# Output projection: three token tiles first, router sums through the fourth's bank, affine vectors loaded together; last expert pair: factor products behind the statistics

## The chip, the core and the metric

The program runs on one core of a Trainium2 chip. Its time is the device time in microseconds (us), the lower the better; three runs give a median. A traced run records what each engine did: PE (TensorE) multiplies matrices, and PEld is its loading of weights; DVE (VectorE), ACT (ScalarE) and POOL (GpSimd) work elementwise; SP (SyncE) here only issues transfers, which run on 16 DMA engines. The granted clock is the share of TensorE's full clock that the chip let it have.

## What is computed

The trunk has two layers over 512 tokens of 1024 numbers, and both end in the same kind of expert block. The part that matters is the end of the second mixer, its router and the experts behind it:

```
mix = (h * gelu(gate_br)) @ w_out                     # [512, 1024] @ [1024, 1024]
x = layer_norm(ALPHA * x + mix, ln_mix_g[1], ln_mix_b[1])
aff = softmax(x @ w_router[1])                        # 16 experts
gates, idx = top_k(aff.T, 64)                         # each expert takes 64 tokens
out_e = (silu(g) * u) @ w_down[e] * gates[e]          # g, u = split(x[idx[e]] @ w_gate_up[e])
x = layer_norm(ALPHA * x + scatter_add(out_e), ln_ffn_g[1], ln_ffn_b[1])
```

The input of the second layer is itself a normalised sum; its factor `ln_ffn_g[0]` and shift `ln_ffn_b[0]` are multiplied and added late, in `affine`, before the residual is taken.

## The kernel before

**Order.** The code is a Python program that emits instructions. Where two of them are independent, a scheduler in the compiler sets their order on each engine from costs of its own; each engine then runs its own list strictly in order, and waits at the head of it for whatever the head needs. `after(i, j)` puts `i` behind `j` by hand. Inside the expert pairs (from the second on) PE's order is the code's.

**Tiles.** Tokens lie in four tiles of 128 (`x[t]`, in rows of the trace `z` in the second layer). The accumulators of PE come from `bank(tag)`: four banks `A`, two `B`, two `C`, used in rotation.

**Output projection** (in `rglru`). The eight 128-row slices of `w_out` (`kk` in `ks`) are each split into a high and a low part (`wh` by ACT, `wl` by DVE), and each of the eight accumulators `acc[t, hf]` (tile, half of the columns; `wops` in rows) takes three products per slice: 192 in all. Before the change all eight accumulators get their banks at once, the first four slices go over all tiles, and then tile after tile takes its last four slices. DVE meanwhile does `affine`: it multiplies the four tiles by one vector, and adds the other. Both vectors pass through one buffer, `ffnvec`, so the second load (`ln_ffn_b`) is issued when the four products are done.

**Router.** `Router.prepare` transposes the vectors of the mixer's norm (`mixT`), scales the router's weights by them, and lets PE sum the columns (`rsums`); it is put behind the last product of the first four slices, and takes two `C` banks. `Router.finish` follows for each tile: statistics on DVE (`ln_mv`), eight transposes on PE (`rtp`), copies, the eight products with the router's weights (`logits`, two rows of the trace for each), and on DVE and ACT the softmax (`lg`, then the exponential on ACT, then `aff`). When all four tiles have their `aff`, `Router.first` ranks the tokens of the first two experts: `affb` on PE, four counting passes `junk` on DVE, then the selection matrix `oh`. With it PE gathers tokens (`gather`) and starts the first gate and up products (`gu`).

**Experts** (`moe`). Eight pairs of experts. Each pair reads 24 MB of weights, all issued on SP's list in one order; a load waits until the buffer that it goes to was read by PE. Some buffers of the first pair are the former `hgh` tiles of the output projection (`wgu000`, `wgu001`, `wgu100`, `wgu101`).

**Last pair.** The outputs are added half by half, and the last half in two quarters: `down` (`yp`), `weigh` (`ysb`, its high part on ACT, its low part on DVE), `spread` (`comb`), and on DVE the sum (`acc`) and the statistics (`bn_stats`). `scale` multiplies parts of `acc` by the last norm's factor, which is loaded behind all weights (`grow`). The list `V` of the flow also splits the factor and shift rows (`gbg`) into a high part (`gbgh`, ACT) and a low part (`gbgl`, DVE).

Of the kernel before, what the change touches and what calls it, by code (L numbers as in the profile page):

```python
# [11 lines left out]
F32 = mybir.dt.float32  # L12
# [6 lines left out]
P = 128  # L19
S = 512  # L20
D = 1024
# [12 lines left out]
NEG = -1e30  # L34
W2 = (8, 3)
BACC = {"dynamic_dma_scratch_size": 256}
TAGS = ('AABA', 'BAAB')
LORDER = 'C0 C1 R0 C2 R1 G0 C3 R2 G1 R3 G2 G3'
CONVT = 'BABCBCBB'
CONVE = 'AAAAADDD'  # L40
# [66 lines left out]
def trunk(ctx: ExitStack, tc: tile.TileContext, a: dict, out: bass.AP):  # L107
# [80 lines left out]
    class Router:  # L188
# [4 lines left out]
                nc.sync.dma_start(scratch[8 * i:8 * i + 8, :P], a[f"ln_mix_{nm}"][layer].rearrange("(c p) -> c p", p=P))  # L193
            self.scratch, self.layer = scratch, layer

        def prepare(self, behind=None):
            rows, ones, wb = self.scratch[:16, :P], self.scratch[:, P:2 * P], self.scratch[:, 2 * P:3 * P]
            part = self.scratch[:, 3 * P:3 * P + 2 * NE]
            ps = bank("C", name="mixT")
            mm = nc.tensor.transpose(ps[:, :16], rows, ident[:16, :16])  # L200
            if behind:
                after(mm, behind)
            gb = self.gb = cpool.tile([P, 16], F32, tag="mixT", name="mixT", bufs=2)
            nc.vector.tensor_copy(gb, ps[:, :16])
            nc.gpsimd.memset(ones, 1.0)
            wb = wb.rearrange("p (k e) -> p k e", k=KD)
            for i, w in ((1, wb), (0, self.w)):
                (nc.gpsimd if MIXE[i] == "P" else nc.vector).tensor_tensor(w, self.w, gb[:, i * KD:(i + 1) * KD, None].to_broadcast([P, KD, NE]), op=ALU.mult)
                nc.vector.tensor_reduce(part[:, i * NE:(i + 1) * NE], w.rearrange("p k e -> p e k"), axis=AX.X, op=ALU.add)
            ps = bank("C", name="rsums")[:, :2 * NE]  # L210
            nc.tensor.matmul(ps, ones, part, start=True, stop=True)
            self.sums = cpool.tile([P, 2, NE], F32, tag="rsums", name="rsums", bufs=2)
            nc.vector.tensor_copy(self.sums, ps.rearrange("p (a e) -> p a e", a=2))
            self.aff = cpool.tile([P, NT, NE], F32, tag="aff", name="aff", bufs=2)
            self.rank = cpool.tile([P, NT, 2], F32, tag="rank", name="rank", bufs=2)
# [372 lines left out]
    def rglru(es2, x, normed, w_in, w_r, w_i, w_out, prep):  # L588
        with ExitStack() as es:
# [128 lines left out]
                    nc.vector.tensor_tensor(hl[:, f, :], gt, hh.bitcast(F32)[:, f, :], op=ALU.subtract)  # L718
                hgh[n], hgl[n] = hh, hl

            def affine(pool):
                for nm, op in (("g", ALU.mult), ("b", ALU.add)):
                    v, src = pool.tile([P, D], F32, tag="ffnvec", name="ffnvec", bufs=1), a[f"ln_ffn_{nm}"][0]
                    nc.sync.dma_start(v, bass.AP(tensor=src.tensor, offset=src.offset, ap=[[0, P], [1, D]]))
                    for t in range(NT):
                        nc.vector.tensor_tensor(x[t], x[t], v, op=op)

            for c in LORDER.split():
                {"C": conv_block, "R": lru_block, "G": gate_branch}[c[0]](int(c[1]))
# [8 lines left out]
            for i in hgh:  # L738
                wts[i] = wtile([2, D], f"wout{i}")
                nc.sync.dma_start(wts[i], w_out[256 * i:256 * (i + 1), :].rearrange("(a p) d -> p a d", p=P))  # L740
            router = Router(p1b, alloc(), 1)
            for j, i in enumerate(hgh):
                for h in range(2):
                    ks.append(2 * i + h)
                    wo[2 * i + h] = split(p2 if j < 2 else p1b, wts[i][:, h, :], "A", WOE[2 * j + h], WB if j < 2 else 8)
            acc = {}
            for t in range(NT):
                for hf in range(2):
                    acc[t, hf] = bank("A" if t < 2 else "BC"[t - 2], name="wops")

            def out_mm(t, hf, kk):
                hs, ts_ = slice(hf * 512, (hf + 1) * 512), slice(t * P, (t + 1) * P)
                return mm3(acc[t, hf], hgh[kk // 2][:, kk % 2, ts_], hgl[kk // 2][:, kk % 2, ts_],
                           wo[kk][0][:, hs], wo[kk][1][:, hs], kk == ks[0], kk == ks[-1])

            for kk in ks[:4]:
                for t in range(NT):
                    for hf in range(2):
                        mm = out_mm(t, hf, kk)
            affine(p1b)  # L760
            router.prepare(mm)
            for t in (int(c) for c in TORD):
                for hf in range(2):
                    for kk in ks[4:]:
                        out_mm(t, hf, kk)
                    hs = slice(hf * 512, (hf + 1) * 512)
                    nc.vector.scalar_tensor_tensor(x[t][:, hs], x[t][:, hs], ALPHA, acc[t, hf], op0=ALU.mult, op1=ALU.add)
                router.finish(x[t], t, alloc, TAGS[1][t])
# [3 lines left out]
    def moe(x, layer, w_gu, w_dn, routing, emit):  # L772
        aff = routing.aff
        with ExitStack() as es:
# [5 lines left out]
            for p in range(NPAIR):  # L780
# [108 lines left out]
                for op in flow:  # L889
                    ks, es = ([int(c) for c in w] for w in (op[1:] + ":01").split(":")[:2])  # L890
                    if op[0] == "G":
                        gather(ks, es)
                    elif op[0] == "U":
                        gate_up(ks, es)
                    elif op[0] == "X":
                        tail = ks
                    elif op[0] == "W":
                        combine_weights()
                    elif op[0] == "C":
                        combine(ks)  # L900
                    elif op[0] == "P":
                        routing.positions(sel[0])
                    elif op[0] == "V":
                        grow = xpool.tile([P, D], F32, tag="act", name="grow", bufs=NT)
                        rows = xpool.tile([P, D], F32, tag="act", name="gbg", bufs=NT)[:3]
                        gbg = [xpool.tile([P, D], F32R, tag="act", name="gbg" + s, bufs=NT)[:3] for s in "hl"]
                        gsrc, bsrc = (a[f"ln_ffn_{nm}"][1] for nm in "gb")
                        end = after(nc.sync.dma_start(grow, bass.AP(tensor=gsrc.tensor, offset=gsrc.offset, ap=[[0, P], [1, D]])), end)
                        for i, src in enumerate((gsrc, bsrc, gsrc)):
                            end = after(nc.sync.dma_start(rows[i:i + 1, :], src.rearrange("(o d) -> o d", o=1)), end)  # L910
                        nc.scalar.copy(gbg[0], rows)
                        nc.vector.tensor_tensor(gbg[1], rows, gbg[0].bitcast(F32), op=ALU.subtract)
                        mcol = cpool.tile([P, NT, 3], F32, tag="mixT", name="mcol", bufs=2)
                        nc.gpsimd.memset(mcol, 1.0)
                h = gpool.tile([P, FF], F32, tag="hy", name="h", bufs=2)
# [63 lines left out]
                if last:  # L979
# [9 lines left out]
                    for i, (n, cols) in enumerate(((0, slice(0, 512)), (1, halves[0]))):  # L989
# [4 lines left out]
                        for t in range(NT):  # L994
                            ps = bank("C", name="comb")[:, :cols.stop - cols.start]
                            spread(ps, t, n, cols)
                            nc.vector.tensor_tensor(acc[t][:, ns], acc[t][:, ns], ps, op=ALU.add)
                            nc.vector.bn_stats(sts[t][:, i, :], acc[t][:, ns])
                        for t, j in (((0, 0), (1, 0)), ((0, 1), (1, 1), (2, 1), (3, 1), (2, 0)))[i] if emit else ():
                            scale(t, (slice(0, 512), slice(512, 768))[j])  # L1000
                    down(1, range(KD), halves[1])
                    weigh(1, halves[1])
                    for t in range(NT):
# [93 lines left out]
```

## Time and profile before

| what | value |
|---|---|
| median of 3 runs | 1405.56 us (1404.56 to 1405.69) |
| the traced execution | 1406.57 us, of which 1404.8 us from the first to the last instruction |
| share of that span busy | PE 96%, DVE 41%, ACT 25%, POOL 5% |
| chain of work that ended last | PE 82%, DMA 10%, DVE 4%, ACT 3% |
| mean granted TensorE clock | 0.977 |

The chain is followed back from the last instruction: at each step it goes to whatever released it. A row of the timeline merges neighbours of one kind: start, length, engine, line, operation, output and input tiles, count, and in brackets the idle time ahead of it with its releaser.

### The profile page before, as it was taken

The numbers are of one execution on the slowest core, as the hardware profiler recorded it, in microseconds if no ns is written. First come the engines' busy times: TensorE is split into PE (matmuls) and PEld (weight loads), VectorE is DVE, ScalarE is ACT, GpSimd is POOL, SyncE is SP. The second block draws the span as 40 slices with busy tenths as digits, with TensorE's granted clock in tenths as the row PEclk, the third lists the DMA queues.
The fourth block names the chain that finished last, engine by engine and source line by source line (L and its number), as shares of the span: only waits on it lengthen the run. The fifth ranks groups of instructions, "written<-read, shape, count | busy, mean of one in ns | idle before, by whom it ended". The sixth has DMA issues, their size and how long they took to land.

```text
span 1404.8 us, 17589 instructions
## 1 busy us (share of the span) xinstructions
PE 1354.5 (96%) x7015; PEld 770.4 (55%) x7015; DVE 574.4 (41%) x1293; ACT 345.7 (25%) x671; POOL 66.6 (5%) x105
## 2 busy tenths in 40 slices
PE   7998998999999999999799999999999999999996
PEld 7986776453453553544466668854553543544533
DVE  4586868232220230211556887762240211212206
ACT  5455332111010010110336883211010110111110
POOL 3142320000000000000000000000000000000000
PEclk9999998999999999999899999889999999999997
DMA  5134357979999999999931327648999999999992
GB/s 189 64 82 129 142 225 285 367 323 421 420 419 421 421 420 421 420 421 409 376 105 60 119 91 270 275 171 346 377 420 420 420 420 420 419 420 420 420 388 96
DMA packets 93095, 437.31 MB, mean 311 GB/s; under 512 B 10315, under 2 KB 37203, under 8 KB 46422
## 3 DMA queue, kind: packets, MB, share of 16 engines
q1 hardware_dynamic: 93014, 436.20, 78.0%
q8 instruction: 55, 0.90, 0.3%
q14 instruction: 26, 0.21, 0.0%
HBM read 434.07 MB, written 2.10 MB: 310 GB/s over the span
## 4 chain that ended last, share of the span: by engine, by line
PE 82%; DMA 10%; DVE 4%; ACT 3%; issue 1%; SPq 0%; POOL 0%; ACTq 0%; DVEq 0%; POOLq 0%
PE gu L867 28%; PE yp L952 14%; PE gather L851 8%; DMA wgu<-in_moe_w_gate_up_dram 4%; DMA wdn<-in_moe_w_down_dram 4%; PE comb L964 4%; PE gps L660 3%; PE wops L183 2%; PE wops L185 2%; PE wops L184 2%; PE qkv L185 2%; PE qkv L183 2%; PE qkv L184 1%; PE logits L229 1%; PE po L483 1%; PE htp L928 1%
## 5 line engine op out<-in xcount | busy, mean ns | idle before, releaser
L867 PE MATMUL gu<-wgu,xs 128*64 128x512 f32 x2048 | 460.5, 595 | 1.2 <-ACT xs L857 1.2
L867 PEld LDWEIGHTS gu<-wgu,xs 128*64 128x64 f32 x2048 | 146.5, 137 | 284.1 <-issue 272.8
L952 PE MATMUL yp<-wdn,hT 128*64 128x512 f32 (+1 forms) x1088 | 232.1, 574 | 2.4 <-DMA wdn<-in_moe_w_down_dram 2.4
L921 DVE TENSOR_TENSOR h<-h,gu 128x512 f32<-128x512 f32 x32 | 22.0, 687 | 356.7 <-PE gu L867 305.2
L952 PEld LDWEIGHTS yp<-wdn,hT 128*64 128x64 f32 x1088 | 78.0, 139 | 139.0 <-issue 127.5
L960 DVE SCALAR_TENSOR_TENSOR ysb<-yp,gate,ysb 128x512 fp32r<-128x512 f32 (+1 forms) x34 | 24.4, 719 | 217.5 <-ACT ysb L959 217.5
L920 ACT ACTIVATE h<-gu 128x512 f32<-128x512 f32 x32 | 19.0, 597 | 300.2 <-PE gu L867 300.2
L857 ACT ACTIVATE xs<-gather,mixT 128x128 f32<-128x128 f32 (+1 forms) x74 | 33.5, 455 | 199.5 <-DVE xs L859 134.5
L964 PE MATMUL comb<-ysb,cs 128*128 128x512 f32 (+1 forms) x256 | 68.7, 406 | 7.8 <-DVE ysb L960 3.8
L972 DVE TENSOR_TENSOR acc<-acc,comb 128x512 f32<-128x512 f32 x112 | 71.6, 682 | 0.7
L851 PEld LDWEIGHTS gather<-oh,z 128*128 128x128 f32 x520 | 60.2, 192 | 13.0 <-issue 10.8
L851 PEld LDWEIGHTS gather<-oh,x 128*128 128x128 f32 x520 | 60.3, 192 | 11.7 <-issue 8.9
L959 ACT ACTIVATE ysb<-yp,gate 128x512 fp32r<-128x512 f32 (+1 forms) x34 | 22.5, 662 | 175.1 <-PE yp L952 175.1
L851 PE MATMUL gather<-oh,z 128*128 128x128 f32 (+1 forms) x520 | 62.8, 278 | 1.6 <-DVE oh L829 1.6
L851 PE MATMUL gather<-oh,x 128*128 128x128 f32 (+1 forms) x520 | 63.0, 278 | 0.3 <-DVE pos L326 0.3
L183 PE MATMUL qkv<-wh,xh 128*128 128x256 f32 x192 | 55.3, 289 | 3.6 <-ACT wh L175 3.6
L660 PE MATMUL gps<-xc,wg 128*128 128x512 f32 x128 | 56.5, 593 | 1.5 <-ACT xc L638 1.5
L964 PEld LDWEIGHTS comb<-ysb,cs 128*128 128x128 f32 x256 | 45.6, 192 | 20.8 <-ACT ysb L959 5.5
L185 PE MATMUL qkv<-wh,xl 128*128 128x256 f32 x192 | 56.2, 293 | 0.0
L184 PE MATMUL qkv<-wl,xh 128*128 128x256 f32 x192 | 55.5, 290 | 0.7 <-DVE wl L176 0.7
L859 DVE TENSOR_SCALAR xs<-gather,mixT 128x128 f32<-128x128 f32 x56 | 22.9, 408 | 60.3 <-PE gather L851 60.3
L929 ACT COPY hT<-htp 128x512 f32<-128x512 f32 x32 | 18.7, 585 | 106.1 <-PE htp L928 106.1
(262 smaller groups left out, 1776.1 us busy)
## 6 DMA issues: line engine op xcount, KB each, us to landing
wgu<-in_moe_w_gate_up_dram SPq DMA_DIRECT2D x252, 1024.0 KB, 19.8
wdn<-in_moe_w_down_dram SPq DMA_DIRECT2D x124, 1024.0 KB, 18.9
win<-in_lru_w_in_dram SPq DMA_DIRECT2D x8, 1024.0 KB, 5.5
wqkv<-in_attn_w_qkv_dram SPq DMA_DIRECT2D x12, 512.0 KB, 4.5
wo<-in_attn_w_o_dram SPq DMA_DIRECT2D x16, 256.0 KB, 5.0
wgu<-in_moe_w_gate_up_dram SPq DMA_DIRECT2D x8, 512.0 KB, 4.1
wdn<-in_moe_w_down_dram SPq DMA_DIRECT2D x8, 512.0 KB, 10.5
wout<-in_lru_w_out_dram SPq DMA_DIRECT2D x4, 1024.0 KB, 7.3
```

The costliest lines, as they stand in the source:

```text
L183: nc.tensor.matmul(ps, lh, rh, start=start, stop=False)
L184: nc.tensor.matmul(ps, lh, rl, start=False, stop=False)
L185: return nc.tensor.matmul(ps, ll, rh, start=False, stop=stop)
L660: nc.tensor.matmul(ps, wt[:, 2 * z + gi, kk, fs], xc[n][:, kk, :], start=(kk == 0), stop=(kk == 1))
L851: pe(nc.tensor.matmul(ps[:, i, cols], x[t][:, k * P:(k + 1) * P], oh[:, t, es[0]:es[-1] + 1, :].rearrange("p e s -> p (e s)"), start=(t == ...
L857: nc.scalar.activation(xs[:, k, cols], ps[:, i, cols], AF.Identity, bias=bc, scale=gc)
L859: nc.vector.tensor_scalar(xs[:, k, cols], ps[:, i, cols], gc, bc, op0=ALU.mult, op1=ALU.add)
L867: pe(nc.tensor.matmul(gu[n][e * 64:(e + 1) * 64, :], xs[:, k, e * 64:(e + 1) * 64], wgu[e][k][n // 2][:, n % 2 * 512:(n % 2 + 1) * 512], s ...
L952: pe(nc.tensor.matmul(yp[n][e * 64:(e + 1) * 64, cols], hT[:, k, e * 64:(e + 1) * 64], w, start=(k == 0), stop=(k == KD - 1)))
L960: nc.vector.scalar_tensor_tensor(lo, yp[n][:, cols], gate, hi.bitcast(F32), op0=ALU.mult, op1=ALU.subtract)
L964: pe(nc.tensor.matmul(ps, cs[:, t, :], y[n][:, j, cols], start=start and not j, stop=bool(j)))
L972: nc.vector.tensor_tensor(acc[t][:, ns], acc[t][:, ns], ps, op=ALU.add)
```

## The change

In the output projection a tile's two accumulators get their banks when its first product is emitted, and the first three slices go over tiles 0 to 2 only. Then come `router.prepare` (its transpose behind tile 0's products, its sums behind tile 2's), `affine`, and the same three slices of tile 3; then each tile takes its last five slices. `finish` uses `A` banks for all tiles. Each affine vector has room of its own (the factor whole, the shift in two halves), and the three loads are issued together. Three splits live in the pool `p2`, five in `p1b`, which gets ten slots for eight. In the last pair the factor products that stood behind each piece's sums all go behind the last statistics of the third piece, and `gbgl` moves from DVE to POOL.

```diff
-TAGS = ('AABA', 'BAAB')
+TAGS = ('AABA', 'AAAA')
...
-            nc.tensor.matmul(ps, ones, part, start=True, stop=True)
+            mm = nc.tensor.matmul(ps, ones, part, start=True, stop=True)
+            if later:
+                after(mm, later)
...
-            def affine(pool):
-                for nm, op in (("g", ALU.mult), ("b", ALU.add)):
-                    v, src = pool.tile([P, D], F32, tag="ffnvec", name="ffnvec", bufs=1), a[f"ln_ffn_{nm}"][0]
-                    nc.sync.dma_start(v, bass.AP(tensor=src.tensor, offset=src.offset, ap=[[0, P], [1, D]]))
+            def affine(rows):
+                for v, op in zip(rows, (ALU.mult, ALU.add)):
                     for t in range(NT):
-                        nc.vector.tensor_tensor(x[t], x[t], v, op=op)
+                        for h, part in enumerate(v):
+                            w = D // len(v)
+                            nc.vector.tensor_tensor(x[t][:, w * h:w * (h + 1)], x[t][:, w * h:w * (h + 1)], part, op=op)
...
+            rows = [[p1b.tile([P, D], F32, name="ffnvec")], [alloc() for _ in range(2)]]
+            for nm, v in zip("gb", rows):
+                for h, part in enumerate(v):
+                    src = a[f"ln_ffn_{nm}"][0, D // len(v) * h:D // len(v) * (h + 1)]
+                    nc.sync.dma_start(part, bass.AP(tensor=src.tensor, offset=src.offset, ap=[[0, P], [1, D // len(v)]]))
...
-                    wo[2 * i + h] = split(p2 if j < 2 else p1b, wts[i][:, h, :], "A", WOE[2 * j + h], WB if j < 2 else 8)
+                    wo[2 * i + h] = split(p2 if len(ks) < 4 else p1b, wts[i][:, h, :], "A", "D", WB if len(ks) < 4 else 10)
...
-            for kk in ks[:4]:
-                for t in range(NT):
+            for t in range(NT):
+                if t == NT - 1:
+                    router.prepare(first, mm)
+                    affine(rows)
+                for kk in ks[:3]:
                     for hf in range(2):
                         mm = out_mm(t, hf, kk)
-            affine(p1b)
-            router.prepare(mm)
+                first = mm if t == 0 else first
             for t in (int(c) for c in TORD):
                 for hf in range(2):
-                    for kk in ks[4:]:
+                    for kk in ks[3:]:
                         out_mm(t, hf, kk)
...
-                        nc.vector.tensor_tensor(gbg[1], rows, gbg[0].bitcast(F32), op=ALU.subtract)
+                        nc.gpsimd.tensor_tensor(gbg[1], rows, gbg[0].bitcast(F32), op=ALU.subtract)
...
-                            nc.vector.bn_stats(sts[t][:, i, :], acc[t][:, ns])
-                        for t, j in (((0, 0), (1, 0)), ((0, 1), (1, 1), (2, 1), (3, 1), (2, 0)))[i] if emit else ():
-                            scale(t, (slice(0, 512), slice(512, 768))[j])
+                            seen = nc.vector.bn_stats(sts[t][:, i, :], acc[t][:, ns])
+                    for t, j in ((0, 0), (1, 0), (0, 1), (1, 1), (2, 1), (3, 1), (2, 0)) if emit else ():
+                        after(scale(t, (slice(0, 512), slice(512, 768))[j]), seen)
```

On PE, the end of the output projection stood like this before, from the last transposes of the router's vectors to the ranking (`z_4975` to `z_4978` are the tiles 0 to 3, `wr` the router's weights):

```order
L185 MATMUL wops<-wh,hgl 128x512
L200 MATMUL mixT<-ident,rx 128x16
L229 MATMUL logits<-wr_6040,rx 128x16 x11
L211 MATMUL rsums<-rx 128x32
L229 MATMUL logits<-wr_6040,rx 128x16
L223 MATMUL rtp<-ident,z_4977 128x128 x4
L229 MATMUL logits<-wr_6040,rx 128x16 x4
L223 MATMUL rtp<-ident,z_4977 128x128 x4
L223 MATMUL rtp<-ident,z_4978 128x128 x8
L229 MATMUL logits<-wr_6040,rx 128x16 x16
L275 MATMUL affb<-ident,aff 128x128 x8
```

Now the same stretch, behind the last product of the output projection, reads:

```order
L185 MATMUL wops<-wh,hgl 128x512
L231 MATMUL logits<-wr_6040,rx 128x16 x8
L225 MATMUL rtp<-ident,z_4978 128x128 x4
L277 MATMUL affb<-ident,aff 128x128 x4
L225 MATMUL rtp<-ident,z_4978 128x128 x4
L231 MATMUL logits<-wr_6040,rx 128x16 x4
L277 MATMUL affb<-ident,aff 128x128 x2
L231 MATMUL logits<-wr_6040,rx 128x16 x4
L277 MATMUL affb<-ident,aff 128x128 x2
```

`mixT`, `rsums`, the transposes of tiles 0 to 2 and the logits of tiles 0 and 1 have moved in among the `wops`; of 32 logits 16 are left behind the last `wops`, and of 16 transposes 8.

On SP, between the last slice of `w_out` and the first down weights (`wdn`), the list was:

```order
L740 DMA wout_6037<-in_lru_w_out_dram 128x2x1024
...
L724 DMA ffnvec<-in_ln_ffn_g_dram 128x1024
L787 DMA wgu_6586<-in_moe_w_gate_up_dram 128x2048
L787 DMA wgu_6588<-in_moe_w_gate_up_dram 128x2048
L787 DMA wgu_6592<-in_moe_w_gate_up_dram 128x2048
L787 DMA wgu_6584<-in_moe_w_gate_up_dram 128x2048
L792 DMA wgu_6566<-in_moe_w_gate_up_dram 128x1024
L724 DMA ffnvec<-in_ln_ffn_b_dram 128x1024
L787 DMA wgu_6590<-in_moe_w_gate_up_dram 128x2048
L792 DMA wgu_6567<-in_moe_w_gate_up_dram 128x1024
L809 DMA wdn_6598<-in_moe_w_down_dram 128x2048
```

and is now:

```order
L742 DMA wout_6037<-in_lru_w_out_dram 128x2x1024
...
L748 DMA ffnvec<-in_ln_ffn_g_dram 128x1024
L748 DMA rx<-in_ln_ffn_b_dram 128x512 x2
L795 DMA wgu_6590<-in_moe_w_gate_up_dram 128x2048
L795 DMA wgu_6592<-in_moe_w_gate_up_dram 128x2048
L795 DMA wgu_6594<-in_moe_w_gate_up_dram 128x2048
L795 DMA wgu_6598<-in_moe_w_gate_up_dram 128x2048
L795 DMA wgu_6596<-in_moe_w_gate_up_dram 128x2048
L800 DMA wgu_6572<-in_moe_w_gate_up_dram 128x1024
L817 DMA wdn_6604<-in_moe_w_down_dram 128x2048
```

The shift's load stands right behind the factor's. The half tile `wgu001` (before `wgu_6567`) has gone behind three down weights, and one whole tile, `wgu13`, that before was loaded far earlier, now stands eight places below that first `wdn`. `wgu000` (`wgu_6572`) waits for the `hgh` tile that tile 3's second slice reads last.

On DVE, in the last pair, the list from the second piece's last statistics on was:

```order
L998 BN_STATS ln_st<-acc_6831 128x6
L975 TENSOR_TENSOR acc_6828<-acc_6828,grow 128x512
L975 TENSOR_TENSOR acc_6829<-acc_6829,grow 128x512
L975 TENSOR_TENSOR acc_6830<-acc_6830,grow 128x512
L912 TENSOR_TENSOR gbgl<-gbg,gbgh 3x1024
L960 SCALAR_TENSOR_TENSOR ysb<-yp_8724,gate,ysb 128x256
L997 TENSOR_TENSOR acc_6828<-acc_6828,comb 128x256
```

and is now:

```order
L1006 BN_STATS ln_st<-acc_6837 128x6
L968 SCALAR_TENSOR_TENSOR ysb<-yp_8730,gate,ysb 128x256
L1005 TENSOR_TENSOR acc_6834<-acc_6834,comb 128x256
...
L1006 BN_STATS ln_st<-acc_6837 128x6
L983 TENSOR_TENSOR acc_6834<-acc_6834,grow 128x512
L983 TENSOR_TENSOR acc_6835<-acc_6835,grow 128x512
L983 TENSOR_TENSOR acc_6834<-acc_6834,grow 128x256
L983 TENSOR_TENSOR acc_6835<-acc_6835,grow 128x256
L983 TENSOR_TENSOR acc_6836<-acc_6836,grow 128x256
L983 TENSOR_TENSOR acc_6836<-acc_6836,grow 128x512
L983 TENSOR_TENSOR acc_6837<-acc_6837,grow 128x256
L968 SCALAR_TENSOR_TENSOR ysb<-yp_8730,gate,ysb 128x256
```

`gbgl` is gone from DVE. The seven factor products that this piece and the next had now stand together behind the next piece's statistics and ahead of the last `ysb`.

## Rows read from the trace of the kernel before

**Rows 1.** Stretches: engines' busy us (instructions), granted clock, DMA share, GB/s.

```profile
897.00:1002.00 105.00, 100.68 (x528) 60.68 (x530) 48.31 (x122) 19.36 (x39) 1.19 (x3) 0.90 0.73 291
1002.00:1352.00 350.00, 348.79 (x1804) 158.88 (x1802) 71.13 (x132) 37.56 (x72) 0.00 (x0) 1.00 1.01 420
```

**Rows 2.** PE's waits, 1280 to 1370: us in total, times, longest.

```profile
PE yp L952 <- DMA wdn<-in_moe_w_down_dram: 1.2, 1, 1.2
```

**Rows 3.** SP's waits, 920 to 1060, the longest.

```profile
SPq L809 <- PE gu L867: 58.1, 5, 27.7
```

**Rows 4.** Timeline of PE, from the output projection to the first experts.

```profile
850.56 0.40 PE L183 MATMUL wops<-wh,hgh 128*128 128x512 f32 x1
...
896.26 0.40 PE L185 MATMUL wops<-wh,hgl 128*128 128x512 f32 x1
...
922.05 1.07 PE L851 MATMUL gather<-oh,z 128*128 128x64 f32 x8 [1.57 <-DVE oh L829]
923.62 5.34 PE L867 MATMUL gu<-wgu,xs 128*64 128x512 f32 x8 [0.49 <-ACT xs L857]
...
930.87 3.65 PE L867 MATMUL gu<-wgu,xs 128*64 128x512 f32 x8
```

**Rows 5.** Timeline of PE, the router of the first layer.

```profile
205.09 1.09 PE L223 MATMUL rtp<-ident,x 128*128 128x128 f32 x8
208.81 1.85 PE L229 MATMUL logits<-wr,rx 128*128 128x16 f32 x16
...
213.99 0.40 PE L185 MATMUL wops<-woh,oTl 128*128 128x512 f32 x1
```

**Rows 6.** Timeline of DVE: the first layer's last `aff`; then the second layer.

```profile
224.37 0.23 DVE L239 TENSOR_SCALAR aff<-aff,rst 128x16 f32<-128x16 f32 x1
...
863.50 4.63 DVE L726 TENSOR_TENSOR z<-z,ffnvec 128x1024 f32<-128x1024 f32 x4 [0.74 <-DMA ffnvec<-in_ln_ffn_g_dram]
868.05 1.22 DVE L176 TENSOR_TENSOR wl<-wout,wh 128x1024 fp32r<-128x1024 f32 x1
877.44 4.63 DVE L726 TENSOR_TENSOR z<-z,ffnvec 128x1024 f32<-128x1024 f32 x4 [8.18 <-DMA ffnvec<-in_ln_ffn_b_dram]
...
916.50 0.23 DVE L239 TENSOR_SCALAR aff<-aff,rst 128x16 f32<-128x16 f32 x1
```

**Rows 7.** Stretches, columns as in rows 1.

```profile
925.00:926.00 1.00, 1.00 (x2) 0.23 (x1) 1.00 (x4) 0.00 (x0) 0.00 (x0) 0.50 0.00 0
1382.00:1384.00 2.00, 2.00 (x12) 1.11 (x10) 1.33 (x5) 0.00 (x0) 0.00 (x0) 0.50 0.00 0
```

**Rows 8.** Timeline of DVE, last pair.

```profile
1375.08 1.89 DVE L975 TENSOR_TENSOR acc<-acc,grow 128x512 f32<-128x512 f32 x3 [1.58 <-DMA grow<-in_ln_ffn_g_dram]
1376.89 1.21 DVE L912 TENSOR_TENSOR gbgl<-gbg,gbgh 3x1024 fp32r<-3x1024 f32 x1
1378.02 0.47 DVE L960 SCALAR_TENSOR_TENSOR ysb<-yp,gate,ysb 128x256 fp32r<-128x256 f32 x1
...
1382.58 0.75 DVE L975 TENSOR_TENSOR acc<-acc,grow 128x256 f32<-128x256 f32 x2
1387.25 0.48 DVE L960 SCALAR_TENSOR_TENSOR ysb<-yp,gate,ysb 128x256 fp32r<-128x256 f32 x1 [3.93 <-ACT ysb L959]
```

**Rows 9.** Timelines of ACT and of PE, last pair.

```profile
1374.36 0.47 ACT L959 ACTIVATE ysb<-yp,gate 128x256 fp32r<-128x256 f32 x1 [0.73 <-PE yp L952]
...
1370.64 3.67 PE L952 MATMUL yp<-wdn,hT 128*64 128x256 f32 x32
...
1378.54 2.33 PE L964 MATMUL comb<-ysb,cs 128*128 128x256 f32 x7 [3.27 <-DVE ysb L960]
1380.80 5.89 PE L952 MATMUL yp<-wdn,hT 128*64 128x256 f32 x32
```

**Rows 10.** Writers of one tile, `wol`: count, ns least/median/most, first and last start.

```profile
L511 POOL TENSOR_TENSOR wol<-wo,woh x4: 2381/2388/2412, 133.2 to 146.8; 128x1024 fp32r<-128x1024 f32 x4
L511 DVE TENSOR_TENSOR wol<-wo,woh x4: 1211/1908/4558, 134.1 to 150.8; 128x1024 fp32r<-128x1024 f32 x4
```

More of the change, by code (lines that the diff above doesn't have):

```diff
@@ L194, in __init__, with prepare @@
             self.scratch, self.layer = scratch, layer
-        def prepare(self, behind=None):
+        def prepare(self, behind=None, later=None):
             rows, ones, wb = self.scratch[:16, :P], self.scratch[:, P:2 * P], self.scratch[:, 2 * P:3 * P]
@@ L744, in rglru, with out_mm @@
                     ks.append(2 * i + h)
-                    wo[2 * i + h] = split(p2 if j < 2 else p1b, wts[i][:, h, :], "A", WOE[2 * j + h], WB if j < 2 else 8)
+                    wo[2 * i + h] = split(p2 if len(ks) < 4 else p1b, wts[i][:, h, :], "A", "D", WB if len(ks) < 4 else 10)
             acc = {}
-            for t in range(NT):
-                for hf in range(2):
+            def out_mm(t, hf, kk):
+                if kk == ks[0]:
                     acc[t, hf] = bank("A" if t < 2 else "BC"[t - 2], name="wops")
-            def out_mm(t, hf, kk):
                 hs, ts_ = slice(hf * 512, (hf + 1) * 512), slice(t * P, (t + 1) * P)
@@ L754, in out_mm @@
                            wo[kk][0][:, hs], wo[kk][1][:, hs], kk == ks[0], kk == ks[-1])
-            for kk in ks[:4]:
-                for t in range(NT):
+            for t in range(NT):
[3 more added lines that the diff above has]
+                for kk in ks[:3]:
                     for hf in range(2):
                         mm = out_mm(t, hf, kk)
-            affine(p1b)
-            router.prepare(mm)
+                first = mm if t == 0 else first
             for t in (int(c) for c in TORD):
                 for hf in range(2):
-                    for kk in ks[4:]:
+                    for kk in ks[3:]:
                         out_mm(t, hf, kk)
```

## Prediction, made before the changed kernel ran

> **What bounds the kernel now.** I read the stretches first, since a wait's share of the span says nothing of the stage in which it would pay. From 1002 to 1352 us, six and a half expert pairs, PE is busy for 348.8 of 350 us, and the DMA engines are full at 420 GB/s [rows 1]. Both run side by side, and the waits say who is ahead: PE waited for weights once there, for 1.2 us [rows 2]. So the two are level at the end, and an earlier start of PE helps only if the weights come earlier by as much. Before 1002 they had room: 291 GB/s on the mean from 897 to 1002 [rows 1], and SP's list, which issues them, stood waiting for PE to read its buffers, 58.1 us in five waits of one kind alone [rows 3]. There the loads follow PE. Then I read the two places that the change touches in order of time: the stretch from the last product of the output projection (896.26) to the first gather (922.05) [rows 4], where PE works on small router products and waits at their end for DVE, and the last pair, where it waited 3.27 us for `ysb` [rows 9].
>
> **First part: output projection and router.** No product is removed: 192 `wops` stand in both versions. What moves is what stands behind them. Behind the last one PE had the transposes of tiles 2 and 3 and the logits of all four; now it has those of tile 3, and the logits of tiles 2 and 3.
>
> *The last `wops`.* It ended at 896.26 + 0.40 = 896.66 [rows 4]. Now one more tile's transposes stand ahead of it (1.09 us), two tiles' logits (2 x 1.85) [rows 5], and `mixT` and `rsums`, three small products that I estimate at 0.3. That makes 896.66 + 1.09 + 3.70 + 0.30 = 901.75. It supposes that PE is not held up between. The places where it could be are the weight splits, below, and DVE: tile 0's sums must be ready when PE reaches its transposes. DVE's shift products filled 877.44 to 882.07 because their vector came late, an 8.18 us wait [rows 6]. With both vectors loaded together they can follow the last split at 869.3 and be done near 874; PE reaches tile 0's transposes after 122 of its products, at 0.23 us each from 850.56 (46.1 us less 2.2 for 16 transposes, by 192) near 878.6. So a wait that cost PE nothing goes, and it is what makes room for the early router.
>
> *From there to the last `aff`.* The nearest stretch is the first layer's router, where tiles are also finished among the products: from 213.99 + 0.40 = 214.39 [rows 5] to 224.37 + 0.23 = 224.60 [rows 6], 10.2 us. There three tiles' logits and two tiles' transposes were left, one of each more than here: less 1.85 and 1.09 makes 7.3. Ends: 7.3 and 10.2. I take 8.0, near the lower, with something added because ACT's list has tile 3's normalisation ahead of its exponential. `aff` is then ready at 909.75.
>
> *From there to the gather*, the four counts and `oh`: 916.50 + 0.23 = 916.73 [rows 6] to 922.05 [rows 4], 5.3 us, and nothing of it is changed. Gather at 915.1, a gain of 7.0 (4.8 to 7.7 by the ends).
>
> *The clock.* The first eight `gu` took 5.34 us and the next eight 3.65 [rows 4]; during the first the granted clock fell to 0.50, the level of 1.2 GHz [rows 7]. In the new order PE is thin for some 13 us rather than 25, so the dip may fall elsewhere. If it misses these products that is 1.7 us more; I take half, 0.9, with 0 and 1.7 as ends. First part: **7.9 us, between 4.8 and 9.4**.
>
> *Does it reach the end?* The loads behind the first pair wait for PE and come earlier with it. But the list ahead of them changed: half a tile and a whole one (1.5 MB) now also come behind tile 3's products. From 897 to 1002 there went 105 x 291 GB/s = 30.6 MB; with 1.5 more, at 420 GB/s that takes 76 us. Loading could be through 29 us earlier than it was, and so it doesn't bind a gain of 8. The whole gain passes.
>
> *Transfers and splits.* The shift's two halves are the same 0.5 MB, issued as two. `wh` and `wl` are as many as before, of one size. Ten slots for eight and three splits in `p2` move only which buffer is waited for. I cost them at nothing; what hides them is the lead of the splits over PE, some 3 us (third rival).
>
> **Second part: last pair.** DVE's low half of `ysb` could start when ACT's high half was done, at 1374.36 + 0.47 = 1374.83 [rows 9]. It started at 1378.02, behind three factor products that waited for `grow`, and `gbgl` [rows 8]. Both have left its way: a gain of 3.2 us, and PE's `comb`, which waited 3.27 us for it [rows 9], follows. The sums and statistics of the piece then run as before, 1378.02 to 1382.58 less one pair of factor products (0.7) that stood among them, 3.9 us: done at 1378.7. Then seven factor products: three of 512 columns (1.89 us [rows 8]), four of 256 at half of the 0.75 a pair, 1.5; together 3.4, so DVE is free at 1382.1. PE meanwhile starts its 32 `yp` at 1380.80 - 3.2 = 1377.6. They took 5.89 us because the clock had fallen to 0.50 [rows 7, 9] behind the 3.27 us wait; before, 32 of the kind took 3.67 [rows 9]. Without that wait I expect 3.67: done at 1381.3, ACT's half at 1381.8. So the last `ysb` is set by DVE at 1382.1, for 1387.25 [rows 8]: 5.1 us. If the clock falls all the same it is 1377.6 + 5.9 + 0.5 = 1384.0, 3.2 us. From there on nothing changed. I take **5.0, between 3.2 and 5.3**. `grow` landed by 1375.1 [rows 8], 3.6 us ahead of its first use now.
>
> *`gbgl` on POOL.* It takes at most what POOL's 128x1024 rows of that operation took, 2.39 us for DVE's 1.21 [rows 10]. It is needed by the closing products, over 10 us later. Its danger is DVE: the same rows show DVE's own products of this kind, usually 1.21, take up to 4.56 us while POOL worked on such a tile. The Trainium skill (SBUF — State Buffer, section Who interferes with whom) gives a rule for it: a DVE instruction with two SBUF inputs contends with a GpSimd instruction that reads SBUF, and the loser waits for the whole instruction. The trace agrees with that, by these rows. The factor products have two such inputs; by the rule they would be held if POOL were still at work. POOL should begin by 1373.7 and be through near 1376.1, and they begin at 1378.7: 2.6 us of cover. Without that cover DVE would be late by up to 2.4 us.
>
> **Sum.** 1406.57 - 7.9 - 5.0 = 1393.7 for a traced execution like this one. The three runs have a median 1.0 us below it, 1405.56: so 1392.6. By the ends, 8.0 to 14.7 us of gain: 1397.6 to 1390.9.
>
> **Rivals.**
> - *The weights don't follow.* PE gains at the router, runs into the weights somewhere past 1002, and gives back 7.9 us; the last pair's gain stays: 1400.6. For it: full DMA engines for 350 us. Against: the 29 us of room, and that PE's reads gate the loads up to 1002.
> - *The clock holds.* If the shorter thin stretch of PE keeps the clock up until the gather, the small products in it run at twice the pace; of 13 us perhaps 4 are bound by PE, 2 of which go, with the other 0.8 at the first experts and 0.7 for the shorter `aff` chain: 1392.6 - 3.5 = 1389.1. For it, the shorter stretch; against, that the first layer's router, equally mixed, took its 10.2 us.
> - *The vectors come late* (the other side). DVE's list has the last low split behind the four factor products. PE reads that split near its 95th product, 850.56 + 22 = 872.4; before, it was done at 869.3, the factor having come at 863.50 [rows 6]. Each us beyond 3.1 that the factor comes later stops PE, and with it every tile. The change's gain of 12.9 is gone if it comes 16 us later, at 879.5; at 885 the time is 1411. The shift's load did land only at 877.4, but it was issued behind five loads of weights and the first use of its buffer; the factor stands ahead of these in both lists. A few us of this, not all, would give 1396 to 1400.
> - *No change*: the stretch behind the last `wops` is as long as it was and `comb` is held by something else. It needs both parts to fail.
>
> **Chances.** Forecast as summed, 1390 to 1398: 0.70. Clock holds: 0.10. Weights don't follow, or a part of the late vectors: 0.14, between 1398 and 1402. No change 0.02, slower 0.04. 0.2% of the time, 2.8 us, is about what a measurement here can tell from no change: faster 0.94, same 0.02, slower 0.04. The range 1388.0 to 1399.0 leaves out the slower half of the third case and the rest.
>
> **What would show it.** Right: the first gather near 915, the last `aff` near 910, `wops` without a wait on DVE or ACT; the full DMA stretch beginning some 8 us earlier, with PE's waits for weights past it still near 1 us; in the last pair no wait of DVE for `grow`, the 32 last `yp` in 3.7 us, the last `ysb` some 5 us nearer to the start of the pair's `gu`. Wrong: waits of `wops` for a split; waits of `yp` or `gu` for weights of 5 us and more; factor products on DVE far over 0.7 us, or the last `ysb` waiting for them.

## Result, and the profile after

The changed kernel took **1391.57 us** (median of 4 runs, 1390.44 to 1394.48), beside 1405.06 us for the kernel before (4 runs): ratio 0.9912, 95% interval 0.989 to 0.9934. The forecast was 1392.6 us, between 1388 and 1399. The execution that was traced took 1391.36 us, its span is 1389.5 us, the mean granted clock 0.985.

Timeline of PE after, from the output projection to the first experts, answering to [rows 4]; start, duration, engine, line, operation, in brackets the idle time ahead of it:

```profile
850.30 0.40 PE L183 MATMUL wops<-wh,hgh 128*128 128x512 f32 x1
...
901.14 0.39 PE L185 MATMUL wops<-wh,hgl 128*128 128x512 f32 x1
901.37 1.85 PE L231 MATMUL logits<-wr,rx 128*128 128x16 f32 x16
903.07 0.63 PE L225 MATMUL rtp<-ident,z 128*128 128x128 f32 x4
...
909.18 0.71 PE L277 MATMUL affb<-ident,aff 128*128 128x128 f32 x4 [2.00 <-DVE aff L241]
909.73 2.88 PE L284 MATMUL idle<-ident 128*128 128x128 f32 x16
912.40 1.06 PE L313 MATMUL affps<-ident,aff 128*16 128x128 f32 x4
913.69 1.20 PE L859 MATMUL gather<-oh,z 128*128 128x64 f32 x8 [0.23 <-DVE oh L837]
915.38 3.87 PE L875 MATMUL gu<-wgu,xs 128*64 128x512 f32 x8 [0.49 <-ACT xs L865]
```

The last product ends at 901.53 (forecast 901.75), and no `wops` waited for anything. The gather starts at 913.69 (915.1), 8.4 us earlier than before. Timeline of DVE, answering to [rows 6]:

```profile
863.26 4.62 DVE L728 TENSOR_TENSOR z<-z,ffnvec 128x1024 f32<-128x1024 f32 x4
867.81 1.22 DVE L176 TENSOR_TENSOR wl<-wout,wh 128x1024 fp32r<-128x1024 f32 x1
868.94 1.89 DVE L728 TENSOR_TENSOR z<-z,rx 128x512 f32<-128x512 f32 x3
...
908.90 0.23 DVE L241 TENSOR_SCALAR aff<-aff,rst 128x16 f32<-128x16 f32 x1
```

The 8.18 us wait for the shift is gone, and the last `aff` is ready at 909.13 (909.75).

Stretches after (columns as in [rows 1]: PE, PEld, DVE, ACT, POOL, clock, DMA share, GB/s):

```profile
897.00:925.00 28.00, 25.27 (x138) 17.93 (x137) 22.56 (x67) 6.21 (x14) 1.53 (x5) 0.94 0.92 359
897.00:990.00 93.00, 90.06 (x496) 51.25 (x496) 46.26 (x111) 16.99 (x35) 1.53 (x5) 0.98 0.88 349
1002.00:1340.00 338.00, 336.78 (x1750) 155.03 (x1748) 71.09 (x132) 37.58 (x72) 0.00 (x0) 1.00 1.01 420
```

Behind the router the picture is that of before, only earlier: PE busy nearly all the time, and from 1002 on the DMA engines full. PE's wait for weights there (total, times, longest, in us) is that of [rows 2], but for the line number:

```profile
PE yp L960 <- DMA wdn<-in_moe_w_down_dram: 1.2, 1, 1.2
```

The last pair, timelines of DVE, PE and POOL, answering to [rows 8, 9]:

```profile
1365.29 0.48 DVE L968 SCALAR_TENSOR_TENSOR ysb<-yp,gate,ysb 128x256 fp32r<-128x256 f32 x1 [1.37 <-ACT ysb L967]
...
1368.90 3.21 DVE L983 TENSOR_TENSOR acc<-acc,grow 128x512 f32<-128x512 f32 x7
1372.04 0.47 DVE L968 SCALAR_TENSOR_TENSOR ysb<-yp,gate,ysb 128x256 fp32r<-128x256 f32 x1
...
1367.49 3.67 PE L960 MATMUL yp<-wdn,hT 128*64 128x256 f32 x32
...
1363.86 2.34 POOL L920 TENSOR_TENSOR gbgl<-gbg,gbgh 3x1024 fp32r<-3x1024 f32 x1 [456.10 <-ACT gbgh L919]
```

DVE waits for ACT's half alone, the 32 `yp` take 3.67 us instead of 5.89, and DVE, with its seven factor products, sets the last `ysb`.

### Three distances that separate the parts

To compare executions I cut each trace at the same three places and subtract: **A** from the start of the first `wops` to the end of the first eight `gu` (after: 915.38 + 3.87 - 850.30), **B** from there to DVE's first `h` product of the last pair (L929 after, L921 before; 1343.48), **C** from there to the end of the span. "Before's order" and "after's order" say which order the router has.

| kernel | A | B | C |
|---|---|---|---|
| before | 78.40 | 424.10 | 51.74 |
| before's order: e2, e6 | 73.55, 73.42 | 423.94, 423.93 | 46.04, 52.28 |
| after | 68.95 | 424.23 | 46.02 |
| after's order: e1, e3, e4, e7 | 70.14, 71.66, 68.94, 72.20 | 424.21, 424.04, 424.27, 424.22 | 51.04, 46.27, 51.23, 46.03 |
| router's sums late: e9 | 79.31 | 424.08 | 46.06 |
| one vector buffer: e5, e13 | 69.16, 69.49 | 424.15, 424.16 | 46.00, 45.96 |
| filled waits: e12 | 68.96 | 424.04 | 46.01 |
| extra copy: e10, e11 | 68.96, 70.14 | 427.83, 430.75 | 45.79, 45.81 |

Column A is the first part, C the second, and B what lies between. Ahead of A stands the start of the first `wops`, where nothing was changed: it lies between 848.42 and 851.97 in these traces, a scatter of 3.6 us that no column holds.

### The profile page after: what moved, and what is told of

The parts are those of the page before. It is cut to its first block, busy times and chain, and to the rows that moved or that the text cites. A ratio compares the mean times of both kernels' runs of the same rounds, so it can differ in the third digit from the quotient of the medians.

```text
span 1389.5 us, 17585 instructions
## 1 busy us (share of the span) xinstructions
PE 1344.2 (97%) x7015; PEld 761.3 (55%) x7015; DVE 572.9 (41%) x1296; ACT 346.1 (25%) x671; POOL 69.1 (5%) x106
## 4 chain that ended last, share of the span: by engine, by line
PE 80%; DMA 13%; DVE 4%; ACT 3%; issue 1%; SPq 0%; POOL 0%; ACTq 0%; DVEq 0%; POOLq 0%
PE gu L875 28%; PE yp L960 12%; PE gather L859 8%; DMA wgu<-in_moe_w_gate_up_dram 6%; DMA wdn<-in_moe_w_down_dram 5%; PE comb L972 3%; PE gps L662 3%; PE wops L183 2%; PE wops L185 2%; PE wops L184 2%; PE qkv L185 2%; PE qkv L183 2%; PE qkv L184 2%; PE po L485 1%; DMA win<-in_lru_w_in_dram 1%; PE htp L936 1%
## 5 line engine op out<-in xcount | busy, mean ns | idle before, releaser
L929 DVE TENSOR_TENSOR h<-h,gu 128x512 f32<-128x512 f32 x32 | 22.0, 688 | 356.8 <-PE gu L875 305.3
```

## Experiments

Where a diff is given it is against the changed kernel, unless it says "before". Medians are set against that kernel's 1391.57 us. A ratio is to runs of the kernel before that were taken beside the experiment; their medians lay between 1403.7 and 1405.15 us, so a difference of two medians can be off by some 1.5 us, and the ratios are the safer numbers.

**e1, the first part alone.** Second part undone:

```diff
-                            seen = nc.vector.bn_stats(sts[t][:, i, :], acc[t][:, ns])
-                    for t, j in ((0, 0), (1, 0), (0, 1), (1, 1), (2, 1), (3, 1), (2, 0)) if emit else ():
-                        after(scale(t, (slice(0, 512), slice(512, 768))[j]), seen)
+                            nc.vector.bn_stats(sts[t][:, i, :], acc[t][:, ns])
+                        for t, j in (((0, 0), (1, 0)), ((0, 1), (1, 1), (2, 1), (3, 1), (2, 0)))[i] if emit else ():
+                            scale(t, (slice(0, 512), slice(512, 768))[j])
...
-                        nc.gpsimd.tensor_tensor(gbg[1], rows, gbg[0].bitcast(F32), op=ALU.subtract)
+                        nc.vector.tensor_tensor(gbg[1], rows, gbg[0].bitcast(F32), op=ALU.subtract)
```

> The change without its second part: the factor products stand where they stood before, gbgl is DVE's again. Theory (the two parts are independent and the router's gain passes whole to the end): about 9.5 us below the kernel before and some 4 to 5.6 above the whole change, 1395.5 to 1397.5 us; first gather near 913.7, the first gu of the last pair 9.6 us earlier than before, and in the last pair the picture of before: DVE's low ysb some 3.2 us later behind the factor products and gbgl, the 32 yp behind it near 5.9 us. Rival (the weights do not follow): 1400 to 1405 us, with waits of yp or gu for weights of 5 us and more. Rival (only both together help): within 3 us of the kernel before.

Measured: 1398.44 us (1396.32 to 1399.17), ratio 0.9951 (0.9938 to 0.9964). The gain, 6.9 us (5.1 to 8.7), is below the 9.5 that I expected and near the 7.9 of the forecast. A is 70.14, B as everywhere, C 51.04 as before: the gain reaches the end whole.

**e2, the second part alone**: the same lines, the other way, in the kernel before.

> The kernel before with the second part alone: factor products behind the statistics, gbgl on POOL. Theory: 5.0 to 5.6 us below the kernel before, 1399.5 to 1400.3 us, with no DVE wait for grow, the 32 yp in 3.7 us and the first 1345 us of the trace as before. Rival (the second part helps only because the last pair starts at another moment): within 2 us of the kernel before.

Measured: 1399.13 us (1395.74 to 1401.29), ratio 0.9956 (0.9941 to 0.997): 6.2 us, and C is 46.04. The product of both ratios is 0.9907, the whole change has 0.9912: the parts add. But the traced execution, 1396.35 us, differs from the kernel before also where nothing was changed. Its timeline of PE, and one stretch of it (columns as in [rows 1]):

```profile
919.06 1.08 PE L851 MATMUL gather<-oh,z 128*128 128x64 f32 x8 [1.33 <-DVE oh L829]
920.63 3.99 PE L867 MATMUL gu<-wgu,xs 128*64 128x512 f32 x8 [0.49 <-ACT xs L857]
...
909.00:911.00 2.00, 2.00 (x20) 2.00 (x20) 0.64 (x3) 1.15 (x2) 0.00 (x0) 1.00 1.01 426
```

The same stretch in the trace of before:

```profile
909.00:911.00 2.00, 2.00 (x11) 2.00 (x11) 0.00 (x0) 1.21 (x2) 0.00 (x0) 0.50 1.01 426
```

With the same order of instructions, A is 73.55 instead of 78.40: the clock, at 0.50 from 901 to 917 in the trace of before, came back between in e2. So "the first 1345 us as before" failed, and the difference of these two traces is the clock's.

**e3, `gbgl` back on DVE** (the one line of e1's second piece).

> The whole change with gbgl back on DVE, ahead of the low ysb. Theory (the low ysb is set by ACT's high half, which ends 1.5 us after gbgh, and a gbgl of 1.21 us fits in between): at most 0.5 us above the whole change, 1391.4 to 1392.2 us, yp still 3.7 us. Rival (moving gbgl is what frees DVE): 1.2 us later at ysb, and if the clock then falls 2.2 us more at yp: 1392.8 to 1395 us.

Measured: 1392.70 us (1390.68 to 1394.57), ratio 0.9912 (0.9899 to 0.9925), the same as the whole change. Timeline of DVE:

```profile
1367.07 1.21 DVE L920 TENSOR_TENSOR gbgl<-gbg,gbgh 3x1024 fp32r<-3x1024 f32 x1 [0.49 <-ACT gbgh L919]
1368.21 0.47 DVE L968 SCALAR_TENSOR_TENSOR ysb<-yp,gate,ysb 128x256 fp32r<-128x256 f32 x1
```

`gbgl` fits between `gbgh` and the low `ysb`; C is 46.27, 0.25 us longer. With the factor products gone, moving it is worth no more than that, which the runs can't tell from nothing.

**e4, the factor products back** (the first piece of e1's diff); `gbgl` stays on POOL.

> The whole change with the factor products back at their old places; gbgl stays on POOL. Theory (the factor products' wait for grow is what held the low ysb): DVE's low ysb some 2 us later than in the whole change, the clock falls behind PE's wait and the 32 yp take 5 to 5.9 us: 3.5 to 5 us above the whole change, 1395 to 1396.5 us. Rival (gbgl was it): at most 1 us above the whole change, 1391.5 to 1392.5 us.

Measured: 1397.65 us (1395.41 to 1398.59), ratio 0.9945 (0.9933 to 0.9957), 6.1 us above the whole change; C is 51.23, 5.2 us longer. Timelines of DVE, POOL and PE:

```profile
1366.57 2.91 DVE L983 TENSOR_TENSOR acc<-acc,grow 128x512 f32<-128x512 f32 x3 [1.56 <-DMA grow<-in_ln_ffn_g_dram]
1369.41 0.47 DVE L968 SCALAR_TENSOR_TENSOR ysb<-yp,gate,ysb 128x256 fp32r<-128x256 f32 x1
...
1365.39 2.33 POOL L920 TENSOR_TENSOR gbgl<-gbg,gbgh 3x1024 fp32r<-3x1024 f32 x1 [456.58 <-ACT gbgh L919]
...
1372.18 5.57 PE L960 MATMUL yp<-wdn,hT 128*64 128x256 f32 x32
```

The three products took 1.89 us before [rows 8] and 2.91 here, where they started while POOL was at `gbgl` (to 1367.72): of the 1.21 us that DVE saved on `gbgl` it lost 1.02 beside it. This is the contention that the forecast priced, and the cover of the whole change avoids it. By the Trainium skill (SBUF — State Buffer, section Who interferes with whom) a DVE instruction with two SBUF inputs contends with a GpSimd instruction that reads SBUF; the trace agrees: the first of the three took 1.71 us, to 1368.28, and the other two 0.68 each.

**e5, one buffer for both vectors**, as before; the router's order stays.

```diff
-            rows = [[p1b.tile([P, D], F32, name="ffnvec")], [alloc() for _ in range(2)]]
...
-            def affine(rows):
+            def affine(pool):
+                for nm, op in (("g", ALU.mult), ("b", ALU.add)):
+                    v, src = pool.tile([P, D], F32, tag="ffnvec", name="ffnvec", bufs=1), a[f"ln_ffn_{nm}"][0]
...
```

> The whole change, but with one buffer for both affine vectors, as before: the shift is loaded when the factor has been used, behind five loads of weights, and DVE's shift products wait for it until near 877 and end near 882, while the order of the router among the products stays. Theory (the joined load is what makes room for the early router): tile 0 is ready 8 us later, its transposes fall behind tile 1's products, about one tile's transposes and logits more stand behind the last wops (2.9 us): 1393 to 1396 us. Rival (the load has slack enough): within 1 us of the whole change, 1391 to 1392.5 us. Rival (the load is the gain): all of the first part lost, 1398 us and more.

Measured: 1389.61 us (1388.78 to 1393.35), ratio 0.9897 (0.9881 to 0.9914). My theory fell. Timelines of PE and DVE:

```profile
875.48 0.30 PE L211 MATMUL rsums<-rx 128*128 128x32 f32 x2
887.04 1.04 PE L225 MATMUL rtp<-ident,z 128*128 128x128 f32 x8
...
877.00 4.63 DVE L728 TENSOR_TENSOR z<-z,ffnvec 128x1024 f32<-128x1024 f32 x4 [0.99 <-DMA ffnvec<-in_ln_ffn_b_dram]
...
909.51 0.23 DVE L241 TENSOR_SCALAR aff<-aff,rst 128x16 f32<-128x16 f32 x1
```

The shift came late and tile 0's transposes moved from 878.56 to 887.04, but PE took products meanwhile; counted from the first `wops` (here 851.89) the last `aff` starts at 57.6, in the whole change at 58.6. More small products stood behind the last `wops`, and passed at full clock up to 909. This traced execution is the slowest of the four (1393.35 us), so that the trace does not show where a lower median would come from.

**e6, the joined load alone**: in the kernel before, `affine` and its loads as in the whole change.

> The kernel before with only the joined load of the affine vectors. Theory (DVE's wait of 8.18 us cost PE nothing as long as the router's sums come last): the wait is gone, tiles are finished a little earlier, and the last aff and the gather stand where they stood: 1403.5 to 1405.5 us. Rival (this wait held the router): 3 us and more below the kernel before.

Measured: 1403.84 us (1401.79 to 1406.51), ratio 1.0007 (0.9996 to 1.0019). The load alone gives nothing, as the theory said.

**e9, the sums late**: three slices first and the joined load, but

```diff
             for t in range(NT):
                 if t == NT - 1:
-                    router.prepare(first, mm)
                     affine(rows)
                 for kk in ks[:3]:
                     for hf in range(2):
                         mm = out_mm(t, hf, kk)
-                first = mm if t == 0 else first
+            router.prepare(mm)
```

> The whole change, but the router's sums and the scaled weights come behind all products of the first part, so that they have to wait for the fourth tile's bank: three tiles' logits and their tails stand behind the last wops again. Theory (what the first part gains is that mixT and rsums get through before the fourth tile): last wops near 897 again, the last aff some 15 to 20 us behind it, the first gather 7 to 9 us later than in the whole change: 1398 to 1401 us. Rival (the order of three slices for each tile, or the joined load, is the gain): within 2 us of the whole change.

Measured: 1401.61 us (1399.19 to 1405.12), ratio 0.9986 (0.9975 to 0.9997), 10 us above the whole change. Timeline of PE:

```profile
895.66 0.23 PE L200 MATMUL mixT<-ident,rx 16*128 16x16 f32 x1
898.03 1.96 PE L231 MATMUL logits<-wr,rx 128*128 128x16 f32 x16 [2.14 <-DVE ln_mv L142]
...
924.37 1.14 PE L858 MATMUL gather<-oh,z 128*128 128x64 f32 x8
```

`mixT` takes a `C` bank, by the code one of those that the fourth tile now holds, and it stands behind the last `wops`; so do the logits of all tiles, and PE worked through most of them at a clock of 0.50, from 901 to 923: A is 79.31. The second part is in this version, and alone it has a ratio of 0.9956 (e2): without the early sums nothing is left of the first part, though the order of three slices, the pools and the joined load are all in it.

**e7, no idle products** while DVE counts: `WARM = (6, 0)` for `(6, 8)`.

> The whole change without the eight products (16 rows) that PE works off into an unused bank while DVE counts. Theory (the gather waits for the counts and oh, not for PE; the products only hold the clock up): the gather at the same distance from the first wops, 63.4 us, the granted clock at 0.5 during the first gu, which take 5.3 to 6.5 us for 3.9: 0 to 2.5 us above the whole change, 1391.5 to 1394 us. Rival (these products, at half clock, are on the way to the gather): 0.5 to 1.5 us below the whole change.

Measured: 1393.51 us (1392.95 to 1395.09), ratio 0.9929 (0.9914 to 0.9944). Timeline of PE, and one stretch:

```profile
912.13 1.97 PE L859 MATMUL gather<-oh,z 128*128 128x64 f32 x8 [3.60 <-DVE oh L837]
914.60 6.35 PE L875 MATMUL gu<-wgu,xs 128*64 128x512 f32 x8 [0.49 <-ACT xs L865]
...
915.00:917.00 2.00, 2.00 (x3) 0.46 (x2) 2.00 (x7) 0.00 (x0) 0.00 (x0) 0.50 1.02 422
```

The gather stands 63.38 us behind the first `wops`, in the whole change 63.39: there DVE's counts set it. The clock fell while PE waited for them, and the first `gu` ran at 0.50 (last row, a stretch), 6.35 us for 3.87. But the rival also has a case: in e1 and e11, where the idle products themselves ran at 0.50, the gather waited for nothing and stood at 64.16, so there they held it up by 0.8 us. And in e3, with the products, the first `gu` took 6.47 us all the same. Whether they pay is open: the intervals of e7 and of the whole change overlap.

**e10, a copy early.** Four copies of 128 rows (2.1 MB) from the weights to the output, which the last writes overwrite, in SP's list behind the second pair's `wgu`:

```diff
...
+                for i in range(4) if emit and p in (1,) else ():
+                    after(nc.sync.dma_start(out[0, P * i:P * (i + 1), :], w_gu[2 * p, P * i:P * (i + 1), :D]), loads[-1])
```

> The whole change with 2 MB more to move: four copies of 128 weight rows into the output, which the last writes overwrite, in SP's list among the loads of the second expert pair, near 930 us. Theory (before 990 us the loads follow PE and the DMA engines stand idle in between): within 1 us of the whole change, 1390.5 to 1392.5 us. Rival (every load counts, the weights were the bound from the start): 5.0 us more (2.1 MB at 420 GB/s), or twice that if a copy costs reading and writing: 1396 to 1402 us.

**e11, the copy late**: the same with the fifth pair.

> The same 2 MB in the list among the loads of the fifth pair, behind 1050 us, where the DMA engines are full to the end. Theory (from there on PE and the weights are level, and the lead is used up by the last pairs, where PE waits 1.2 us once): PE waits some 5 us more for weights near the end, 10 if a copy costs reading and writing: 1396 to 1402 us. Rival (there is a lead left): within 1 us of the whole change.

Measured: e10 1394.85 us (1392.85 to 1397.18), ratio 0.9938 (0.9916 to 0.9959); e11 1399.43 us (1396.86 to 1400.02), ratio 0.9964 (0.9949 to 0.9978). Column B grew by 3.6 and by 6.5 us. Waits of the weight loads (PEld) for `wdn`, 930 to 1340, of the whole change, of e10 and of e11 (total, times, longest):

```profile
PEld yp L960 <- DMA wdn<-in_moe_w_down_dram: 3.0, 3, 2.1
```

```profile
PEld yp L962 <- DMA wdn<-in_moe_w_down_dram: 5.5, 5, 2.1
```

```profile
PEld yp L962 <- DMA wdn<-in_moe_w_down_dram: 9.5, 8, 2.1
```

In e11 the copy was issued at 1145 to 1153, and it went as the theory says: no lead is left. e10 did not, and came out between its theory and its rival. The copy was issued at 966 and not near 930. Of the 6.5 us that the same copy cost late, 2.9 were absorbed there (of the 5.0 us that 2.1 MB take at 420 GB/s, 1.4). Its stretch from 960 to 965 shows why it was not more: the DMA engines were nearly idle, but SP's list stood at the loads ahead of the copy, which waited for PE.

```profile
960.00:965.00 5.00, 5.00 (x26) 1.72 (x24) 2.39 (x4) 0.00 (x0) 0.00 (x0) 1.00 0.09 31
```

**e12, the waits filled**: eight products into an unused bank behind the last `logits`, and twelve for eight at `WARM`.

> The whole change with products into an unused bank in two places where PE waits: eight between the last logits and the last tile's affb (2.0 us wait for aff), and twelve instead of eight while DVE counts. Theory (the granted clock falls because PE has little to do there, and only the first gu pay): the clock stays at 1.0 through the first gu more often, gather at the same distance of 63.4 us from the first wops: 0 to 2 us below the whole change, 1389.5 to 1391.5 us. Rival (the added products come in the way of affb and affps): 0.5 to 2 us above it.

Measured: 1391.55 us (1389.24 to 1392.16), ratio 0.9905 (0.9888 to 0.9923). The stretch of the router, for 0.94 in the whole change:

```profile
897.00:925.00 28.00, 26.37 (x164) 19.69 (x161) 22.59 (x71) 6.48 (x14) 1.54 (x5) 1.00 0.90 352
```

In this trace the clock held all through, and nothing was won: the gather is at 63.39 us again, A at 68.96.

**e13, one buffer and filled waits**, four products and twelve.

> The version with one vector buffer (1389.6 us), with four products between the last logits and affb and twelve for eight while DVE counts. Theory (as for the version before): 1388 to 1389.5 us, the lowest of all versions. Rival (the products come in the way): 1390 to 1392 us.

Measured: 1391.46 us (1391.26 to 1392.78), ratio 0.991 (0.9894 to 0.9926). Neither better nor worse than the whole change: the theory's 1388 to 1389.5 us missed. The filling did not hold the clock here, for the first eight `gu` took 5.34 us in the trace. e5 has the lowest median, but its interval overlaps the whole change's, so no version here is shown to beat it.

## Why the prediction was right, step by step

- **The first part.** The steps came out within 0.7 us up to the last `aff`, and 1.4 us early at the gather, which is set 4.6 us behind `aff` instead of 5.3. Between the two traces A shrank by 9.45 us, above my upper end of 9.4; over the runs of e1 the part is worth 6.9 (5.1 to 8.7), for 7.9 forecast. The traces differ more because the one of before caught a long stretch at half clock; the same order took 73.5 in e2 and e6.
- **What makes it.** The early sums are needed, shown by e9: without them nothing of the part is left. A sentence of the working was wrong: the joined load "is what makes room for the early router". e6 shows that it gives nothing alone, e5 that the order does without it. No term of the sum hung on it. The rival of late vectors did not appear; e5 made the shift late and cost nothing.
- **The clock.** I gave this rival 0.10 and 1389.1 us. It came true in half: in the trace after, the clock is 0.94 on the mean from 897 to 925, where it was 0.68 from 897 to 929 before, and the small products ran at full clock up to 909. Where it falls moves from run to run, with 71.66 in e3 (first `gu` 6.47 us) and 68.94 in e4 for one and the same order.
- **Passing to the end.** Right, and stronger than I argued: B is 423.9 to 424.3 in all twelve traces without a copy, whatever A was. SP's list shows the loads following PE: the down weights that were issued at 1034.48 before went out at 1024.77 after, 9.7 us earlier. The room that I gave as reason, 29 us, was wrong as a size: it took a mean rate for a reserve. At 966 a copy that cost 6.5 us late found 2.9. The idle time of the DMA engines before 990 is in large part the list waiting for PE's reads; a load that stands behind a waiting one can't use it, but for the same reason it moves along when PE moves. How much would fit near 900, where the 1.5 MB went, and whether another queue could use the idle time, was not tried.
- **The second part.** 5.0 us forecast; C shrank by 5.7, and e2's runs give 6.2 (4.2 to 8.3). The size is off at the statistics: 1365.29 to 1368.90 is 3.6 us, where I had 3.9, and the seven factor products took 3.2 for 3.4. The mechanism was right in order and price: e4 shows that the products, with their wait for `grow`, held the low `ysb`, and that the clock came down behind PE's wait for it (0.50 from 1370 to 1376), 5.2 of the 5.7 us; `gbgl` alone is 0.25 (e3).
- **The sum.** 6.9 + 6.2 = 13.1 by the parts' runs, 13.5 by the medians, 12.9 in the forecast's sum. By the parts' runs I had the first part 1.0 us too high and the second 1.2 too low, both within what the runs can tell: that the sum is so near is in part luck. Between the traced executions the gain is 15.2; A accounts for the rest, 9.45 there for 6.9 in e1's runs.

## What to carry to other kernels

A product that needs an accumulator bank which a later tile holds comes behind that tile, and all that needs its result does too: place it before the tile takes the bank. Before you price a wait that goes, ask what was due behind it: an 8.18 us wait of DVE was worth nothing here, one of 1.58 us in front of PE's last chain, with what followed it, over 5. And whether an early gain lasts is not told by the mean rate of the DMA engines but by whom the list of loads waits for; a distance between two late marks, taken in several runs, tells it at once.

## What the runs showed of the hardware

The granted clock stood at 0.50, the level of 1.2 GHz, in stretches in which PE shows as busy all the time with small products (before, 901 to 917, behind a wait of 2.23 us for `ln_mv` up to 899.05), and for the same instructions it fell at other places in other runs: A moved from 73.4 to 78.4 us in before's order and from 68.9 to 71.7 in after's. A single pair of traces is uncertain here by some 3 to 5 us, nearly what the second part is worth. A copy of 2.1 MB from memory to memory cost 6.5 us in the one trace where the DMA engines were full (e11, column B), between the 5.0 us of one passage at 420 GB/s and twice that.
